# Load order of the last four summed weight tiles in a hybrid attention block

## The chip, the core and the metric

The kernel runs on one core of one Trainium2 chip. The metric is the time of one execution in microseconds (us) as the device reports it; the median of several executions stands for a kernel. A profile shows one execution on that core: PE is TensorE with its matmuls (PEld its weight loads), DVE is VectorE, ACT is ScalarE, POOL is GpSimd, and SP is the engine whose queue starts almost every DMA here.

## What is computed

The reference is one encoder layer: one input projection, two kinds of attention, gating, an output projection and a layer norm. Cut to what matters:

```python
h = x @ w_in                      # x (1024, 1024), w_in (1024, 3328)
q_a, k_a, v_a, z_a, q_b, k_b, v_b, z_b = split(h)
y_a = neighborhood_attention(q_a, k_a, v_a, rel_pos_bias)   # 8 heads of 64, 8 x 16 window on a 16 x 64 grid
y_b = windowed_gqa_with_sink(rotary(q_b), rotary(k_b), v_b, sink_logits)  # 8 query heads, 2 key heads, |i-j| <= 128
mixed = concat([y_a * silu(z_a), y_b * silu(z_b)])
x = layer_norm(2 ** 0.25 * x + mixed @ w_out, ln_gain, ln_bias)
```

## The kernel before

Accuracy comes from splitting float32 operands into a high and a low 16-bit part and adding three products. To split a weight tile the kernel must first know a power-of-two scale that keeps it in range, and that scale comes from sums of absolute values. This bookkeeping is what the change touches.

**Tiling.** The columns of `w_in` other than the values are cut into 21 column tiles of 128 columns, in the order of the list `ORDER`. Each tile is projected for two halves of the 1024 tokens, with 8 blocks of 128 rows and three products each: 48 matmuls of 128x512, line 401. The value columns are projected at the start in float32 (line 482).

**Two sorts of tiles.** The first six (`NPRO`, the names `zb0, z0, zb1, kb, qb0, z1`) are projected in the prologue, each with a scale of its own: as they are loaded (`wr`, line 192), ACT scans each half of a tile (`w_scan`, line 233), and `w_scale` turns the sums into the scale with a small matmul against a matrix of ones (lines 248 and 250) and five small DVE instructions (251 to 255). For the gate tiles among them (`ZPRO`, the tiles 0, 1, 2 and 5) sums by single column are needed too: `z_tree` adds up the scanned copies on DVE (lines 238 to 240) before the matmul of line 248.

The other 15 tiles (`NS`) are projected later, between the attention's own matmuls, and share one scale. So the prologue loads all of them as `ws0` to `ws14` (`sum_load`, line 641, 512 KB each), and sums their absolute values (`sum_w`): on ACT at line 670, on ACT at line 663 for the four gate tiles in `ZSUM` = 1, 5, 13 and 14, whose scanned copies go into the buffer `junk` that `w_scan` uses too, and on DVE at line 659 for tiles 4 and 7. The last eight tiles (`NR`) stay in their buffers and are split from there, much later (lines 203, 208 and 209); the others are loaded again when their turn comes.

**What sets the order.** In the prologue the program is written out by hand: `run_to` counts matmuls of line 401, and `at(c, fn)` puts a piece of work behind matmul number c. The sums stand at 14, 28, and so on up to 210, one for every 14 matmuls. Each sum, when it is placed, issues the load that stands four further on in the list of loads; the first four loads stand ahead of all sums. An engine executes its instructions in the order of the program, and so does the SP queue: a load behind a waiting one waits with it. The sum places run over the tiles 0 to 10 and then 13, 11, 14, 12, by a small table in the line that places them. The loads run over 0 to 14. The scale of the common group is computed behind matmul 219 from all 15 sums.

**Buffers.** The tiles `ws` rotate through eight buffers of the pool tag `big2`. Eight later tiles take the same buffers in the same rotation: four pairs of split output weights (`wo`, line 989) and the split gated results `m` of four head pairs (line 1015). A later tile waits until the last reader of the tile in its buffer is done.

Of the kernel before, what the change touches and what calls it, by code (L numbers as in the profile page):

```python
# [31 lines left out]
NS = 21 - NPRO  # L32
ZPRO = (0, 1, 2, 5)
ZSUM = (1, 5, 13, 14)
DSUM = (4, 7)
NR = 8
FILL = ORDER[NPRO:]
FILL_AT = [0, 8, 17, 25, 33, 41, 49, 57, 66, 74.5, 82.5, 91, 99, 107, 114, 121.5, 124, 126, 128, 131, 136]
# [27 lines left out]
def hybrid_block(ctx, tc, xT, x, wt, wv, wo, bias, sink, gain, lbias, cos, sin, bmask, out):  # L66
# [20 lines left out]
    def big_tile(name, shape=(128, 2, 512), dt=F32R):  # L87
        n = taken[0]
        taken[0] += 1
        tag = "big" if n < 8 or 16 <= n < 24 or n >= 32 + NS else "big2"  # L90
        return big.tile(list(shape), dt, tag=tag, name=name)
# [94 lines left out]
    NH = 2 * len(ORDER)  # L186
    NL = NH - 2 * NR

# [36 lines left out]
    def z_abs(n):  # L225
        return junk[:, S * (zabs[n] % 2):S * (zabs[n] % 2) + S]
# [206 lines left out]
    with ExitStack() as vctx:  # L433
# [201 lines left out]

        sums = {}

        def sum_load(i):
            if i < NS:
                sums[i] = big_tile(f"ws{i}", (128, 2, 4, 128), F32)  # L640
                nc.sync.dma_start(sums[i], wt[NPRO + i].rearrange("h p k c -> p h k c"))

# [7 lines left out]
            j = ZSUM.index(n - NPRO)  # L650
            nc.vector.tensor_reduce(zc[:, j:j + 1], zps.pop(n)[:, :128], axis=AXX, op=ALU.max)

        def sum_w(i):
            t, c = sums[i].rearrange("p h k c -> p (h k c)"), 2 * NPRO + i
            if i >= NS - NR:
                for h in range(2):
                    raws[2 * (NPRO + i) + h] = sums[i][:, h]
            if i in DSUM:
                nc.vector.tensor_reduce(wm[:, c:c + 1], t, axis=AXX, op=ALU.add, apply_absolute_value=True)
            elif i in ZSUM:  # L660
                n = NPRO + i
                zabs[n] = len(zabs)
                nc.scalar.activation(z_abs(n), t, AF.Abs, accum_out=wm[:, c:c + 1])
                if i == ZSUM[-1]:
                    at(ran[0] + 70, z_tree, n)
                else:
                    for d, fn in ((23, z_tree), (47, z_sum), (51, z_max)):
                        at(ran[0] + d, fn, n)
            else:
                nc.scalar.activation(scrap, t, AF.Abs, accum_out=wm[:, c:c + 1])  # L670
            sum_load(i + 4)

        def at(c, fn, *a):
            events.setdefault(c, []).append(lambda: fn(*a))
# [43 lines left out]
        for i in range(4):  # L718
            sum_load(i)
        for i in range(NS):  # L720
            at(14 + 14 * i, sum_w, {11: 13, 12: 11, 13: 14, 14: 12}.get(i, i))
        at(219, w_scale, NPRO)
        fill.extend(project(n) for n in ORDER[:NPRO])
        run_to(100)
# [139 lines left out]
    def quad(q):  # L864
        g, p, j, t, _ = units[4 * q]
        return g, p, j, t // 4 if g == "b" else t[0] // 2
# [315 lines left out]
    for i in range(-LD, NU + LO):  # L1182
# [61 lines left out]
        if 0 <= q < NU // 4:  # L1244
            g, p, j, h = quad(q)
# [90 lines left out]
```

## Time and profile before

| | |
|---|---|
| median of 3 runs | 449.64 us (449.15 to 450.77) |
| the profiled execution | 449.93 us, span from first to last instruction 448.1 us |
| PE busy | 439.5 us, 98% of the span |
| DVE, ACT, POOL busy | 344.6 us (77%), 304.1 us (68%), 229.3 us (51%) |
| HBM traffic over the span | 140 GB/s |
| granted TensorE clock, mean | 0.996 |

The profiled execution's own time is 1.8 us more than its span: that lies before the first and behind the last instruction. PE is nearly always busy, so where PE is kept waiting matters more than how busy the rest is. The ends of matmuls are modelled, 0.38 us for one of 128x512 where the next one starts 0.22 us after it, so a short stall of PE can hide in a busy row; starts are safer to read.

### The profile page before, as it was taken

To read this page: it belongs to the slowest core of one execution; us is meant where nothing else is said; L and a number is where in the kernel's file an instruction comes from. 1 tells how busy PE (TensorE), PEld (TensorE's weight loads), DVE (VectorE), ACT (ScalarE), POOL (GpSimd) and SP (SyncE) were. 2 spreads that over 40 slices of the span, in tenths; PEclk is the share of its full clock that TensorE was granted. 3 is DMA by queue.
4 is the path that set the end of the run, shared out by engine and by line. 5 is a ranking of instruction groups with operands and counts; after the bars stand their busy time and mean duration, and the time that the engine had idled before them with its cause. 6 is when DMAs were issued, how large, how long until landed. Compare 5 with 4: busy or idle time off the path is not lost.

```text
span 448.1 us, 9544 instructions
## 1 busy us (share of the span) xinstructions
PE 439.5 (98%) x3269; PEld 262.8 (59%) x3269; DVE 344.6 (77%) x857; ACT 304.1 (68%) x704; POOL 229.3 (51%) x244
## 2 busy tenths in 40 slices
PE   8999999998999999999999999999999999999994
PEld 8999974443445555565655565656555654444442
DVE  5787987927989787786898888897777746179954
ACT  5638749858578998888988978797886886002211
POOL 0003942563837838868516729667753555005840
PEclk9999999999999999999999999999999999999998
DMA  8897377985848888887888999999999878101721
GB/s 249 285 313 275 96 255 241 279 280 197 304 148 166 146 153 164 173 141 136 163 161 185 177 191 193 191 181 236 195 193 226 157 191 325 49 0 70 248 82 70
DMA packets 135136, 83.86 MB, mean 187 GB/s; under 512 B 101424, under 2 KB 113456, under 8 KB 134832
## 3 DMA queue, kind: packets, MB, share of 16 engines
q1 hardware_dynamic: 134656, 82.77, 75.8%
q8 instruction: 25, 0.41, 0.4%
q10 hardware_dynamic: 432, 0.49, 0.3%
q14 instruction: 23, 0.19, 0.1%
HBM read 52.83 MB, written 9.96 MB: 140 GB/s over the span
## 4 chain that ended last, share of the span: by engine, by line
PE 87%; POOL 4%; issue 4%; DMA 3%; DVE 1%; SPq 1%; ACT 1%; POOLq 0%; ACTq 0%; DVEq 0%
PE ps_pj L401 39%; PE ps_s L1033 9%; PE ps_t L886 7%; PE ps_s L482 6%; PE ps_pj L1033 5%; PE ps_t L1033 5%; PE ps_s L821 4%; PE ps_s L822 4%; PE ps_pj L482 3%; PE ps_t L482 3%; POOL wl L209 2%; PE ps_t L906 2%; DMA ws<-in_wt 1%; DMA wvraw<-in_wv 1%; POOL wr L208 1%
## 5 line engine op out<-in xcount | busy, mean ns | idle before, releaser
L401 PE MATMUL ps_pj<-xf,wh 128*128 128x512 f16 x672 | 202.6, 379 | 0.0
L401 PE MATMUL ps_pj<-xf,wl 128*128 128x512 f16 x336 | 127.3, 379 | 0.0
L401 PEld LDWEIGHTS <-wh 128*128 128x128 f16 x672 | 63.8, 98 | 61.7 <-issue 1.8
L847 ACT ACTIVATE ps_s<-sn,nm 128x385 f32<-128x385 f32 (+3 forms) x128 | 70.0, 547 | 29.6 <-DVE nm L831 28.6
L858 DVE SCALAR_TENSOR_TENSOR split<-ps_s,split 128x384 f16<-128x384 f32 (+2 forms) x128 | 65.6, 512 | 17.2 <-ACT split L857 16.3
L1033 PEld LDWEIGHTS <-m 128*128 128x128 f16 x408 | 38.8, 98 | 42.7 <-issue 0.2
L857 ACT ACTIVATE split<-ps_s 128x384 f16<-128x384 f32 (+2 forms) x128 | 57.6, 450 | 2.4
L401 PEld LDWEIGHTS <-wl 128*128 128x128 f16 x336 | 32.9, 98 | 36.7
L831 DVE CUSTOM_DVE_ANT_0 sn<-ps_s,bias,sg 128x264 f32<-128x264 f32 (+1 forms) x64 | 35.2, 550 | 16.0 <-PE ps_s L822 5.9
L208 POOL TENSOR_SCALAR wr<-wr,wsc 128x512 f32<-128x512 f32 x26 | 21.8, 840 | 42.4 <-ACT wh L203 36.8
L1033 PE MATMUL ps_s<-wo,m 128*128 128x512 f16 (+1 forms) x192 | 42.0, 372 | 0.0
L831 DVE CUSTOM_DVE_ANT_0 sn<-ps_s,bm,nsk 128x384 f32<-128x384 f32 (+1 forms) x64 | 40.7, 636 | 1.5 <-PE ps_s L822 1.3
L793 POOL TENSOR_SCALAR bias<-bias,rsg 128x552 f32<-128x552 f32 (+1 forms) x24 | 18.7, 779 | 40.2 <-DMA bias<-in_bias 35.4
L821 PE MATMUL ps_s<-ks,qs 128*128 128x384 f16 (+4 forms) x128 | 39.2, 306 | 0.0
L822 PE MATMUL ps_s<-ks,qs 128*128 128x384 f16 (+4 forms) x128 | 39.2, 306 | 0.0
L886 PEld LDWEIGHTS <-tr 128*128 128x128 f16 (+1 forms) x1104 | 36.6, 98 | 2.2
L209 POOL TENSOR_TENSOR wl<-wr,wh 128x512 f16<-128x512 f32 x26 | 32.2, 1240 | 2.2
L1090 ACT ACTIVATE sd<-mv,eps 128x1 f32<-128x1 f32 x8 | 2.4, 295 | 45.1 <-DVE mv L1088 42.8
L1132 POOL TENSOR_TENSOR xr<-xr,gb 128x512 f32<-128x512 f32 x7 | 11.2, 1607 | 41.1 <-ACT xr L1129 41.1
L482 PE MATMUL ps_s<-wvh,x 128*128 128x320 f32 x128 | 29.4, 310 | 0.0
L315 POOL COPY ks<-ks 64x512 f16<-64x512 f16 x40 | 26.0, 662 | 4.7 <-DVE ks L285 1.8
L1033 PE MATMUL ps_pj<-wo,m 128*128 128x512 f16 (+1 forms) x120 | 25.2, 347 | 0.0
(187 smaller groups left out, 827.8 us busy)
## 6 DMA issues: line engine op xcount, KB each, us to landing
xraw<-in_xT SPq DMA_DIRECT2D x31, 256.0 KB, 4.4
ws<-in_wt SPq DMA_DIRECT2D x15, 512.0 KB, 5.2
wr<-in_wt SPq DMA_DIRECT2D x26, 256.0 KB, 3.0
bias<-in_bias SPq DMA_DIRECT2D x16, 276.0 KB, 3.5
wor<-in_wo SPq DMA_DIRECT2D x16, 256.0 KB, 3.3
xr<-in_x SPq DMA_DIRECT2D x8, 512.0 KB, 9.0
out<-xr SPq DMA_DIRECT2D x14, 256.0 KB, 2.1
bias<-in_bias SPq DMA_DIRECT2D x8, 368.0 KB, 3.8
```

The lines of the kernel that those rows point to most:

```text
L208: nc.gpsimd.tensor_scalar(raw, raw, scale, 1.0, op0=ALU.mult, op1=ALU.mult)
L209: nc.gpsimd.tensor_sub(l, raw, h)
L401: nc.tensor.matmul(ps, a[:, k % 4, :], mv, start=(k == 0 and i == 0), stop=(k == KT - 1 and i == 2))
L482: nc.tensor.matmul(ps[:, :320], lh[t // 4, k][:, ts], rh[k][:, cs], start=(k == 0 and i == 0), stop=(k == KT - 1 and i == 2))
L821: nc.tensor.matmul(ps[:, :m], q, sl[0], start=True, stop=False)
L822: nc.tensor.matmul(ps[:, :m], q, sl[1], start=False, stop=True)
L831: nc.vector.tensor_tensor_reduce(sn[:, :m], ps[:, :m], bias_t, sg[:, c:c + 1], init, op0=ALU.add, op1=ALU.min, accum_out=nm)
L847: nc.scalar.activation(pt[:, :m], sn[:, :m], AF.Exp, bias=nm, scale=-1.0, accum_out=sm[:, k:k + 1])
L857: nc.scalar.activation(hl[:, :m, 0, :c], src, AF.Copy, scale=PSCALE)
L858: nc.vector.scalar_tensor_tensor(hl[:, :m, 1, :c], src, PSCALE, hl[:, :m, 0, :c], op0=ALU.mult, op1=ALU.subtract)
L886: nc.tensor.matmul(ps[:, HD * m:HD * m + HD], a, b_, start=(i == 0), stop=(i == len(mms) - 1))
L1033: nc.tensor.matmul(ps, lh[:, ts], rh[:, cs], start=(e == EO[0] and i == 0), stop=(e == EO[-1] and i == 2))
```

## The change

The order of the sums becomes a list, `SUMS`, and both the loads and the sums go through it. Before, the places of the sums were permuted and the loads were not.

```diff
+SUMS = list(range(11)) + [13, 11, 14, 12]
...
-        def sum_load(i):
-            if i < NS:
+        def sum_load(j):
+            if j < NS:
+                i = SUMS[j]
                 sums[i] = big_tile(f"ws{i}", (128, 2, 4, 128), F32)
                 nc.sync.dma_start(sums[i], wt[NPRO + i].rearrange("h p k c -> p h k c"))
...
-        def sum_w(i):
+        def sum_w(j):
+            i = SUMS[j]
             t, c = sums[i].rearrange("p h k c -> p (h k c)"), 2 * NPRO + i
...
-            sum_load(i + 4)
+            sum_load(j + 4)
...
         for i in range(NS):
-            at(14 + 14 * i, sum_w, {11: 13, 12: 11, 13: 14, 14: 12}.get(i, i))
+            at(14 + 14 * i, sum_w, i)
```

A second effect lies in the old `sum_load(i + 4)`: its argument was the tile's number, not the place of the sum. For the sums of tiles 0 to 10 the two are the same, and these issue all remaining loads, so no load is added or lost.

On SP, at the place where the last of these loads are issued, the kernel before has these rows (`ws` are the summed tiles with their numbers, `wr` halves of the prologue's tiles, `vwin` a copy of the values in device memory; a number behind the underscore is that of the buffer object, in the order of allocation):

```order
L641 DMA ws10_1125<-in_wt 128x2x512
L192 DMA wr12_1171<-in_wt 128x512
L641 DMA ws11_1178<-in_wt 128x2x512
L641 DMA ws12_1199<-in_wt 128x2x512
L641 DMA ws13_1219<-in_wt 128x2x512
L192 DMA wr13_1238<-in_wt 128x512
L641 DMA ws14_1252<-in_wt 128x2x512
L192 DMA wr14_1262<-in_wt 128x512
L738 DMA vwin0_76<-vd_75 64x6144
```

And this is the same place with the change (its line numbers are up to three higher):

```order
L643 DMA ws10_1125<-in_wt 128x2x512
L193 DMA wr12_1171<-in_wt 128x512
L643 DMA ws13_1178<-in_wt 128x2x512
L643 DMA ws11_1199<-in_wt 128x2x512
L643 DMA ws14_1219<-in_wt 128x2x512
L193 DMA wr13_1238<-in_wt 128x512
L643 DMA ws12_1252<-in_wt 128x2x512
L193 DMA wr14_1262<-in_wt 128x512
L741 DMA vwin0_76<-vd_75 64x6144
```

The queue has the same rows at the same places; four of them carry another tile. Tile 13 goes from the third of the four places to the first, tile 11 from the first to the second, tile 14 from the fourth to the third and tile 12 from the second to the fourth. The buffer objects 1178, 1199, 1219 and 1252, and so the places in the rotation, go with the place in the queue.

On ACT, where these tiles are summed, the kernel before has these rows (`rp_raw` is a projected half tile read out of PSUM for the rotary step, `wh` a high part):

```order
L331 ACTIVATE rp_raw_1276<-ps_pj_1240 128x512
L663 ACTIVATE junk_123,wm_108<-ws13_1219 128x1024
L233 ACTIVATE junk_123,wm_108<-wr11_1119 128x512
L670 ACTIVATE scrap_128,wm_108<-ws11_1178 128x1024
L331 ACTIVATE rp_raw_1327<-ps_pj_1280 128x512
L203 ACTIVATE wh10_1330<-wr10_1032,wsc_110 128x512
```

And with the change:

```order
L332 ACTIVATE rp_raw_1276<-ps_pj_1240 128x512
L666 ACTIVATE junk_123,wm_108<-ws13_1178 128x1024
L234 ACTIVATE junk_123,wm_108<-wr11_1119 128x512
L673 ACTIVATE scrap_128,wm_108<-ws11_1199 128x1024
L332 ACTIVATE rp_raw_1327<-ps_pj_1280 128x512
L204 ACTIVATE wh10_1330<-wr10_1032,wsc_110 128x512
```

The order of the sums stands as it was: tile 13, then the scan of the second half of prologue tile 5 (`wr11`), then tile 11. Only the buffers that they read have changed. PE and DVE have the same rows in both kernels.

## The prediction

> **What bounds the kernel now.** I read the page first, then the list of waits of PE and ACT, then the chain of waits around the one wait that mattered, and last the timeline there.
>
> ```profile
> span 448.1 us, 9544 instructions
> PE 439.5 (98%) x3269; PEld 262.8 (59%) x3269; DVE 344.6 (77%) x857; ACT 304.1 (68%) x704; POOL 229.3 (51%) x244
> ...
> PE ps_t L248 <- DVE cs L240: 1.6, 1, 1.6
> PE ps_t L1115 <- ACT dg L1114: 1.5, 1, 1.5
> PE ps_t L441 <- DVE warm L438: 1.0, 1, 1.0
> PE ps_pj L482 <- DVE x L453: 0.3, 1, 0.3
> ...
> ACT junk L663 <- DMA ws<-in_wt: 2.6, 1, 2.6
> ```
>
> PE is the bound: it is busy for 439.5 of 448.1 us. The four PE rows are all its waits on other engines, each with the total, the number of times and the longest. Three belong to the warm-up, the first tiles and the last normalisation, which this change does not touch. The remaining one, 1.6 us at line 248, is a wait in the middle. The ACT row is the only wait of any engine for a `ws` load, 2.6 us, once. The chain of waits ties the two together (start, duration, what):
>
> ```profile
> 94.17 0.43 SPq L641
> ...
> 94.65 0.46 SPq L641
> ...
> 95.15 6.71 DMA ws<-in_wt
> ...
> 103.03 0.62 ACT junk L233 x2
> ...
> 103.67 0.44 DVE junk L238
> ...
> 104.46 0.24 DVE cs L240
> ...
> ```
>
> Three `ws` loads are issued in a row, at 94.17, 94.65 and 95.15. The third is tile 13 and lands at 95.15 + 6.71 = 101.86. ACT then sums it (line 663), scans the last half of prologue tile 5 behind it (line 233), and only then can DVE add up the columns (lines 238 to 240) and PE run the matmul of line 248, with which the chain goes on. So PE's wait is not for the tile that came late: it is for the scan that is queued behind the late tile's sum on ACT.
>
> **What the change moves.** Tile 13's load goes from the third of these places in the SP queue to the first. Tile 11 goes to the second, tile 14 to the third, tile 12 to the fourth, behind a 256 KB load. Nothing is added or removed, all four loads are 512 KB, and SP passes the same number of rows, so the queue itself costs the same. What changes is when each tile lands. The landing of the other places comes from the issues in short stretches of the trace (the last number is us to landing; the stretches hold the first, the second and the fourth place):
>
> ```profile
> ws<-in_wt SPq DMA_DIRECT2D x1, 512.0 KB, 4.5
> ws<-in_wt SPq DMA_DIRECT2D x1, 512.0 KB, 5.9
> 97.26 0.43 SPq L641 DMA_DIRECT2D ws<-in_wt  x1
> ws<-in_wt SPq DMA_DIRECT2D x1, 512.0 KB, 6.7
> ```
>
> First place 94.17 + 4.5 = 98.7, second 94.65 + 5.9 = 100.5, third 101.9, fourth 97.26 + 6.7 = 104.0. In these rows the loads land in the order of issue. I take it that the places keep their landing times, since size and queue are the same: tile 13 then lands at 98.7, 3.2 us earlier.
>
> Now what ends last in its place. The timeline (in brackets the idle time before, and its cause):
>
> ```profile
> 98.69 0.60 ACT L331 ACTIVATE rp_raw<-ps_pj 128x512 f32<-128x512 f32 x1 [1.62 <-PE ps_pj L401]
> 101.88 1.06 ACT L663 ACTIVATE junk<-ws 128x1024 bf16<-128x1024 f32 x1 [2.59 <-DMA ws<-in_wt]
> 101.42 0.69 DVE L335 TENSOR_TENSOR rp_raw<-rp_raw,rp_sw 128x512 f32<-128x512 f32 x1
> 103.67 0.43 DVE L238 TENSOR_TENSOR junk<-junk 128x512 bf16<-128x512 bf16 x1 [1.56 <-ACT junk L233]
> 102.38 0.59 PE L401 MATMUL ps_pj<-xf,wh 128*128 128x512 f16 x2
> 102.81 0.38 PE L401 MATMUL ps_pj<-xf,wl 128*128 128x512 f16 x1
> 104.74 0.22 PE L248 MATMUL ps_t<-cs,ones 128*128 128x128 bf16 x1 [1.55 <-DVE cs L240]
> ```
>
> ACT is free at 98.69 + 0.60 = 99.29, after tile 13 has landed, so the sum starts at 99.29 and the 2.59 us vanish on ACT. From the start of the sum to the start of line 238 it was 103.67 - 101.88 = 1.79 us; the scan would thus let DVE start at 101.08. But DVE is in the rotary step of line 335 until 101.42 + 0.69 = 102.11. **DVE becomes the limit**: it gains 103.67 - 102.11 = 1.56 us, its whole idle time there. From line 238 to the matmul it is 104.74 - 103.67 = 1.07 us, so PE starts line 248 at 102.11 + 1.07 = 103.18. Without any wait it could start 0.22 us after the matmul of 102.81 (the pair at 102.38 takes 0.43 for two starts), at 103.03. PE's true stall of 1.71 us shrinks to 0.15, and the gain is **1.56 us**, bounded above by 1.71.
>
> The other three tiles. The sum of tile 11 followed that of tile 13 by 103.55 - 101.88 = 1.67 us; it would start at 100.96, and its data lands at 100.5, 0.4 us before. If it lands later, ACT waits, at a place where it has time: it next waits for PE. The last two sums, and what uses them:
>
> ```profile
> 103.55 1.04 ACT L670 ACTIVATE scrap<-ws 128x1024 bf16<-128x1024 f32 x1
> ...
> 105.64 0.60 ACT L331 ACTIVATE rp_raw<-ps_pj 128x512 f32<-128x512 f32 x1 [0.96 <-PE ps_pj L401]
> ...
> 108.02 1.06 ACT L663 ACTIVATE junk<-ws 128x1024 bf16<-128x1024 f32 x1
> 109.69 1.04 ACT L670 ACTIVATE scrap<-ws 128x1024 bf16<-128x1024 f32 x1
> 110.63 0.19 ACT L670 ACTIVATION_READ_ACCUMULATOR scrap<-ws 128x1 f32 x1
> ...
> 111.32 0.17 PE L250 MATMUL ps_t<-wm,ones 128*128 128x15 bf16 x1
> ```
>
> All of these follow PE (the row at 105.64 waits for a matmul group), so they move 1.56 us ahead: tile 14 is needed at 106.5 and lands at 101.9, tile 12 at 108.1 and lands at 104.0. Both are covered, by 4 us. The matmul of line 250 keeps its 0.5 us behind the last sum.
>
> **Does the gain reach the end?** No later row of PE's list waits on anything between here and the last normalisation, and there PE is waited for. What could hold it is work that does not move with PE. DMA traffic from before the stall stays where it is, but it has run out before the next loads, as two stretches of 1 us show (the last two columns are DMA share and GB/s):
>
> ```profile
> 106.00:107.00 1.00, 1.00 (x7) 0.44 (x5) 0.93 (x5) 1.00 (x3) 0.06 (x1) 1.00 0.00 0
> 108.00:109.00 1.00, 1.00 (x6) 0.49 (x5) 0.97 (x2) 0.98 (x2) 0.94 (x2) 1.00 0.00 0
> ...
> 123.48 0.63 ACT L430 ACTIVATE scrap<-wos 128x512 bf16<-128x512 f32 x1 [2.82 <-DMA wos<-in_wo]
> 125.74 0.69 DVE L362 SCALAR_TENSOR_TENSOR z<-z,ps_pj 128x512 f32<-128x512 f32 x1
> 126.48 0.59 PE L401 MATMUL ps_pj<-xf,wh 128*128 128x512 f16 x2
> ```
>
> No transfer runs there, so later loads can start 1.56 us earlier. The tight place is 126.48: PE's next group takes the PSUM bank that DVE's line 362 releases at 126.43, 0.05 us before. ACT's wait at 123.48 for a `wos` load stands ahead of it. Since that load is issued behind POOL work that follows ACT and DVE, I take it to move along.
>
> The buffers' later users change too. The third `m` tile now waits for the split of tile 13 instead of tile 11, and the third `wo` pair for tile 14 instead of tile 13:
>
> ```profile
> 317.77 1.16 POOL L209 TENSOR_TENSOR wl<-ws,wh 128x512 f16<-128x512 f32 x1
> 330.90 1.16 POOL L209 TENSOR_TENSOR wl<-ws,wh 128x512 f16<-128x512 f32 x1
> 346.10 0.60 ACT L1015 CAST m<-z 128x512 f16<-128x512 f32 x1
> 361.66 2.55 ACT L989 ACTIVATE wo<-wor,wos 128x512 f16<-128x512 f32 x4
> ```
>
> Tile 13's last split ends at 318.9 and the third `m` is written at 346.1, with 27 us between; tile 14's ends at 332.1 and the `wo` pair is written from 361.7. I cost this at nothing.
>
> **Sum.** The profiled execution took 449.93 us: 449.93 - 1.56 = 448.37. It stands 0.29 above the median of 449.64, so for a median I take 449.64 - 1.56 = **448.1 us**.
>
> [...]
>
> **The rivals.** (1) *The load lands late in its new place.* For: over all 15 loads the time to land goes up to 6.9 us.
>
> ```profile
> DMA to landing us min/median/max: 4.0/5.2/6.9
> ```
>
> With 6.9 us tile 13 lands at 101.07, and the gain is 101.86 - 101.07 = 0.8 us: 448.8 us; as late as now, 449.6. Against: the long landings quoted above are those of the third and fourth place, behind other loads, and the first place has 4.5. (2) *The gain is given back at 126.48.* If the `wos` load ahead of ACT's line 430 keeps its absolute landing, the gate's evacuation and DVE's line 362 stay, and PE waits for its bank what it gained: 449.6 us, no change. Against: the empty DMA queue. (3) *The change does not do what it says to PE*: another wait stands right behind, for example the load of the scan behind the sum; again about 449.6. Against: that load stands ahead of all these in the SP queue, and in the chain the scan's rows come with no wait of their own. (4) *Slower: tile 12 pays.* It now goes last. If it lands after 108.1, ACT's last sum is late, and 0.5 us further on PE's line 250 stalls one for one, and with it all of PE's queue. It decides from a landing at 108.6; the gain is used up at 110.2, and 0.5% of loss needs 112.4, which is 15 us after the issue, against 6.7 in the trace: 452 us or more.
>
> **How the numbers follow.** The forecast gets 0.73, rival (1) 0.10, (2) and (3) together 0.11, (4) 0.06. About 0.5%, or 2.2 us, is what a measurement of this kernel can tell from no change: the three runs before span 1.6 us. The mechanism cannot give 2.2 us, since PE's stall is 1.71; a measured time under 447.4 would take 0.7 us of scatter on top of the forecast, to which I give 0.14. Over 451.9 I give 0.06, from (4). The rest, 0.80, is within 0.5%. The forecast alone would span 447.2 to 448.9; with rivals (1) to (3) the range is 447.2 to 449.8.
>
> **What would show it.** Right: no wait of ACT line 666 (the old 663) for a `ws` load; ACT's sum of tile 13 at about 99.3; DVE's line 238 directly behind its line 336, without idle time; PE's line 249 (the old 248) at about 103.2 and hardly a wait; all of PE 1.5 us earlier from there, and a span near 446.5. Wrong: a wait on ACT for the first of the sums (rival 1), PE's start at 126.48 unmoved (2), a wait of ACT's last sum or PE's line 251 for tile 12 (4), or a gain at 105 us that is gone by 360 us.

## The result, and the profile after

The changed kernel took 448.06 us as a median of 10 runs (447.59 to 450.27), the kernel before 450.24 us in the 10 runs beside it. The ratio is 0.9954, with a 95% interval of 0.9932 to 0.9977: 0.5% faster, where the prediction had 1.56 us or 0.35%. A second set of 12 runs, at a later time, gave 0.9968 (0.9950 to 0.9985).

The waits of PE in the changed kernel (engine and what it waited for; us in total, times, longest):

```profile
PE ps_t L1118 <- ACT dg L1117: 1.5, 1, 1.5
PE ps_t L442 <- DVE warm L439: 1.0, 1, 1.0
```

The wait at line 248 (now 249) is gone. The one ACT wait for a `ws` load has moved to the tile that is summed second, as the view of that tile shows:

```profile
its engine sat idle before it (us, times) until:
  DMA ws<-in_wt: 0.6, 1
who waited for it (us, times):
  ACT scrap L673: 0.6, 1
```

The timeline of the changed kernel at the place that the prediction worked out:

```profile
93.67 1.45 SPq L643 DMA_DIRECT2D ws<-in_wt  x3
...
98.21 0.60 ACT L332 ACTIVATE rp_raw<-ps_pj 128x512 f32<-128x512 f32 x1 [1.62 <-PE ps_pj L402]
98.70 1.05 ACT L666 ACTIVATE junk<-ws 128x1024 bf16<-128x1024 f32 x1
...
99.75 0.61 ACT L234 ACTIVATE junk<-wr 128x512 bf16<-128x512 f32 x1
...
100.93 0.69 DVE L336 TENSOR_TENSOR rp_raw<-rp_raw,rp_sw 128x512 f32<-128x512 f32 x1
...
101.10 1.06 ACT L673 ACTIVATE scrap<-ws 128x1024 bf16<-128x1024 f32 x1 [0.65 <-DMA ws<-in_wt]
...
101.54 0.42 DVE L239 TENSOR_TENSOR junk<-junk 128x512 bf16<-128x512 bf16 x1
...
102.33 0.38 PE L402 MATMUL ps_pj<-xf,wl 128*128 128x512 f16 x1
102.60 0.22 PE L249 MATMUL ps_t<-cs,ones 128*128 128x128 bf16 x1
...
122.15 0.63 ACT L431 ACTIVATE scrap<-wos 128x512 bf16<-128x512 f32 x1 [3.64 <-DMA wos<-in_wo]
```

Tile 13's sum starts right behind the read-out of line 332, without a wait. DVE's line 239 follows line 336 without idle time. PE starts line 249 0.27 us after the matmul ahead of it, 0.05 us more than the usual 0.22.

The whole execution is 2.1 us shorter (spans of 446.0 and 448.1 us), but not all of it is the wait. The row of line 332 is a mark of the same work ahead of the wait: it started at 98.69 before and 98.21 now, so 0.48 us of the difference was there already, from the start of the kernel, where the change does nothing. From this mark to the matmul it was 104.74 - 98.69 = 6.05 us and is 102.60 - 98.21 = 4.39: the wait gave **1.66 us**. Nothing took it back later: from line 248 (now 249) to the end of the span it is 448.1 - 104.74 = 343.4 us before and 446.0 - 102.60 = 343.4 with the change.

### The profile page after: what moved, and what is told of

Read it like the earlier page. It is cut to its first block, busy times and chain, and to the rows that moved or that the text cites. A ratio compares the mean times of both kernels' runs of the same rounds, so it can differ in the third digit from the quotient of the medians.

```text
span 446.0 us, 9544 instructions
## 1 busy us (share of the span) xinstructions
PE 439.2 (98%) x3269; PEld 262.9 (59%) x3269; DVE 344.3 (77%) x857; ACT 303.9 (68%) x704; POOL 229.2 (51%) x244
## 4 chain that ended last, share of the span: by engine, by line
PE 98%; DVE 0%; ACT 0%; issue 0%; ACTq 0%
PE ps_pj L402 49%; PE ps_s L1036 9%; PE ps_t L889 7%; PE ps_s L483 6%; PE ps_pj L1036 5%; PE ps_t L1036 5%; PE ps_s L824 4%; PE ps_s L825 4%; PE ps_pj L483 3%; PE ps_t L483 3%; PE ps_t L909 2%; PE ps_t L442 1%; PE ps_t L1118 0%; DVE xr L1113 0%; ACT xr L1122 0%
```

## The experiments

Each kernel ran beside the kernel before on the same chip; ratios are to that.

**Is it the order of the loads, or the scan behind the sum?** The loads keep their old order, and tile 13's sum is placed one matmul later, behind the scan:

```diff
-            at(14 + 14 * i, sum_w, {11: 13, 12: 11, 13: 14, 14: 12}.get(i, i))
+            at(14 + 14 * i + (i == 11), sum_w, {11: 13, 12: 11, 13: 14, 14: 12}.get(i, i))
```

> The loads keep the old order; only ACT's order changes: the scan of prologue tile 5's last half stands ahead of tile 13's sum. Theory (PE waited for the scan that was queued behind the late sum): ACT still waits about 2 us for tile 13's load, now behind the scan, but PE's wait at line 248 falls from 1.55 us to under 0.3, and the time falls by 1.5 to 2.1 us, ratio to before near 0.996, as with the change. Rival (the order of the loads itself helps, by DMA traffic or otherwise): no gain, ratio 1.000.

Ratio 0.9957 (0.9937 to 0.9977). The timeline of ACT and PE:

```profile
98.80 0.62 ACT L233 ACTIVATE junk<-wr 128x512 bf16<-128x512 f32 x1
...
101.11 1.06 ACT L663 ACTIVATE junk<-ws 128x1024 bf16<-128x1024 f32 x1 [1.60 <-DMA ws<-in_wt]
...
102.70 0.22 PE L248 MATMUL ps_t<-cs,ones 128*128 128x128 bf16 x1
```

ACT still waits for tile 13, 1.6 us, and PE does not wait at line 248 at all. The gain needs no new load order; it needs the scan not to stand behind a late load. The same run shows a wait of PE that the profile of before does not have:

```profile
123.41 0.63 ACT L430 ACTIVATE scrap<-wos 128x512 bf16<-128x512 f32 x1 [5.05 <-DMA wos<-in_wo]
...
124.04 0.67 ACT L361 ACTIVATE z<-ps_pj,invt 128x512 f32<-128x512 f32 x1
...
124.74 0.69 DVE L362 SCALAR_TENSOR_TENSOR z<-z,ps_pj 128x512 f32<-128x512 f32 x1 [1.38 <-ACT z L361]
...
125.48 0.59 PE L401 MATMUL ps_pj<-xf,wh 128*128 128x512 f16 x2 [0.90 <-DVE z L362]
```

It is the same pattern: ACT waits 5.05 us for an output-weight tile, the evacuation of a gate tile stands behind it, DVE's line 362 behind that, and PE waits 0.9 us for the PSUM bank. From line 248 to the end of the span this execution takes 447.1 - 102.70 = 344.4 us, 1.0 more than the 343.4 of the others.

**How early must the tile be?** The loads run through a list of their own, `LOADS`, and the sums as before:

```diff
+LOADS = list(range(11)) + [11, 13, 12, 14]
...
-        def sum_load(i):
-            if i < NS:
+        def sum_load(j):
+            if j < NS:
+                i = LOADS[j]
```

> Tile 13 is loaded in the second of the four places (11, 13, 12, 14). Theory: it lands between the first and the third place, 100.5 by the profile of before and about 1 us later by that of the change, so ACT still waits 1.2 to 2.3 us, PE's wait is 0.1 to 1.3 us, and the gain is a part of the whole, 0.3 to 1.4 us, ratio 0.997 to 0.999. Rival (any landing ahead of the third place gives the whole gain, since DVE is busy until 102.1): ratio 0.9955 and no wait of PE. Rival (the order of the loads does not matter): ratio 1.000 with a wait of 1.5 us.

Ratio 0.9967 (0.9946 to 0.9989). In the profile ACT waits 0.88 us, and PE's line 249 starts at 102.67 without idle time, as with the change:

```profile
99.77 1.06 ACT L665 ACTIVATE junk<-ws 128x1024 bf16<-128x1024 f32 x1 [0.88 <-DMA ws<-in_wt]
...
101.62 0.42 DVE L239 TENSOR_TENSOR junk<-junk 128x512 bf16<-128x512 bf16 x1
...
102.67 0.22 PE L249 MATMUL ps_t<-cs,ones 128*128 128x128 bf16 x1
```

The theory missed: it had 1.2 to 2.3 us of wait for ACT and 0.1 to 1.3 for PE. In this execution the first rival holds: DVE is busy until then, so 0.9 us of lateness is free. The load of the second place landed at 99.75 here and at 101.08 in the profile of the changed kernel, where tile 11 had that place; so late, the scan would have let DVE start at 101.10 + 1.79 = 102.89 there instead of 101.54, and PE would have lost 1.3 us. The intervals do not tell second and first place apart.

**The other way.** The same edit with `[11, 12, 14, 13]`:

> Tile 13 is loaded in the last of the four places (11, 12, 14, 13), the other way from the change. Theory: it lands about 2 us after the third place (104.0 against 101.9), and ACT's scan, DVE and PE move one for one: PE's wait at line 248 is 3.2 to 4.2 us and the time rises by 1.6 to 2.6 us over before, ratio 1.0035 to 1.006. Rival (the gain of the change is not this wait, or PE catches up later): ratio 1.000, or a longer wait without a longer span.

Ratio 1.0092 (1.0064 to 1.0121), 455.11 us: about twice the loss that the theory had. The wait was 4.27 us, just over the range; what was not expected stands in the stretches of 2 us behind it (busy time and instructions of PE, PEld, DVE, ACT and POOL; then the granted clock, DMA share and GB/s):

```profile
104.99 1.06 ACT L665 ACTIVATE junk<-ws 128x1024 bf16<-128x1024 f32 x1 [5.32 <-DMA ws<-in_wt]
107.85 0.27 PE L249 MATMUL ps_t<-cs,ones 128*128 128x128 bf16 x1 [4.27 <-DVE cs L241]
...
104.00:106.00 2.00, 0.00 (x0) 0.00 (x0) 0.00 (x0) 1.01 (x2) 0.00 (x0) 0.99 0.56 236
106.00:108.00 2.00, 0.15 (x2) 0.15 (x2) 0.94 (x3) 1.79 (x6) 0.00 (x0) 0.50 0.03 12
108.00:110.00 2.00, 2.00 (x6) 0.67 (x5) 1.64 (x9) 0.57 (x2) 0.00 (x0) 0.50 0.00 0
110.00:112.00 2.00, 2.00 (x6) 0.76 (x5) 1.93 (x6) 1.95 (x5) 1.19 (x2) 0.50 0.00 0
112.00:114.00 2.00, 2.00 (x9) 0.79 (x8) 1.97 (x2) 2.00 (x4) 1.93 (x2) 0.80 0.03 3
...
116.86 0.17 PE L251 MATMUL ps_t<-wm,ones 128*128 128x15 bf16 x1
```

The granted clock falls to one half and stays there until almost 113. From line 249 to line 251 it is 116.86 - 107.85 = 9.01 us; in the kernel before, the same work from line 248 to line 250 took 111.32 - 104.74 = 6.58. So the stall cost 2.4 us more than its length: PE worked at half the clock from 107.85 to about 112.8, and half of these 4.95 us is 2.5.

**The scatter of the kernel before.**

> The kernel before, unchanged, for a second profile and the scatter. Theory: PE waits at line 248 again, for as long as tile 13 lands late, and that landing differs between executions by about 1 us, so the wait is 1.0 to 3.0 us; ratio 1.000 within 0.25%. If the wait is 1.55 us again to within 0.1, the landing does not scatter, and the 0.5 us by which PE was ahead in the changed kernel before the wait is scatter of the start. If the wait were absent here, the first profile would have been an accident, and the change could not owe its gain to it.

Ratio 0.9979 (0.9958 to 1.0001) between two sets of the same kernel, and a wait of only 0.93 us: under the range expected. In the kernel before's 29 runs beside these, nine had a granted clock of 0.993 or less and took 451.9 to 453.1 us. That raised the question whether these executions, too, had a long wait at line 248.

**Again, with more kernels side by side.**

> The changed kernel, unchanged, beside the other kernels of this job. Theory: no wait of PE at line 249 (old 248) or under 0.3 us, no execution with a granted clock under 0.996, median 447.8 to 448.6 us, ratio to before 0.994 to 0.9975. Rival (the 0.46% of the first comparison was mostly scatter between sets of executions, as the 0.2% between two sets of the kernel before suggests): ratio above 0.9975.

> The kernel before once more, to see its scatter. In the last job 9 of 29 executions of it had a granted clock of 0.992 to 0.993 and took 451.9 to 453.1 us, and none of 12 of the second set. Theory (PE's wait at line 248 is longer in these and halves the clock for some us, as the fourth-place run showed for a wait of 4.3 us): the executions fall into two groups again, those with a clock of 0.996 and more under 451.5 us, those with less above it; a profile of the second group would show a wait over 2.5 us. Rival (the slow group has nothing to do with this wait): such executions occur for the changed kernels in this job as well.

Ratios 0.9968 (0.9950 to 0.9985) and 1.0001 (0.9979 to 1.0022). The changed kernel had no wait of PE at line 249 and no clock under 0.996, a median of 448.29 us. The kernel before had one execution in 12 with a clock of 0.992, at 452.75 us, and in the 34 runs beside it four with 0.993 or less; two more, of 452.4 and 452.6 us in the 29 and the 34 runs, had 0.996, which the split by clock does not explain. The profiled one had a wait of 1.16 us and a mean clock of 0.998.

**Can either late load be kept from PE for good?** First the scan of the output-weight tile alone, moved behind the evacuation, in the changed kernel; then, in a second kernel, also the tile scan ahead of tile 13's sum, as in the first experiment:

```diff
-            at(231 + 10 * i, wo_pre, i)
+            at(276 if i == 3 else 231 + 10 * i, wo_pre, i)
```

> The changed kernel with ACT's scan of the fourth output-weight tile moved from matmul 261 to 276, behind the evacuation of gate tile 5's first half. Theory (the PE wait of 0.9 us seen in the scan-first run, at the PSUM bank behind DVE's line 362, comes from that scan waiting for a late load ahead of the evacuation): ACT still waits for the load, 1 to 4 us, but PE never waits for the bank. In an execution where the load is not late this brings nothing; so the median is 0 to 0.5 us under that of the changed kernel in this job, and the upper end of its times comes down. Rival (the executions of the changed kernel above 449.5 us come from the start of the kernel, where PE waits 0 to 0.6 us for its first tiles): the same median and the same upper end.

> The changed kernel with both scans moved: the scan of prologue tile 5 ahead of tile 13's sum, and the output-weight scan behind the evacuation. Theory: neither late load can reach PE; no PE wait between the first tiles and the last normalisation, the time is that of the changed kernel's good executions, 447.6 to 448.3 us as a median, ratio 0.994 to 0.997. Rival (moving tile 13's sum one place back delays something else, such as the sum of tile 11 and the common scale): a PE wait at line 251 (old 250) or a median above the changed kernel's.

Medians of 448.21 and 448.26 us against 448.29 of the changed kernel beside them; both ratios 0.9960 (0.9944 to 0.9976 and 0.9945 to 0.9976). The upper end of the times stayed near 450 (450.0 and 449.9 against 450.25). Neither is measurably better than the change. In the profile of the first, the gate's evacuation runs 3 us ahead of the scan, and PE has no wait for the bank:

```profile
119.41 0.69 ACT L362 ACTIVATE z<-ps_pj,invt 128x512 f32<-128x512 f32 x1 [0.60 <-PE ps_pj L402]
122.53 0.63 ACT L431 ACTIVATE scrap<-wos 128x512 bf16<-128x512 f32 x1
```

But ACT did not wait for the output-weight load either, in this profile or in the second kernel's, where the theory had 1 to 4 us: at its later place the scan came behind the landing. So these profiles do not show a late load being kept from PE, and the profiles of the changed kernel itself have no wait for the bank. The executions near 450 us must come from elsewhere. The start of the kernel, as the rival has it, was not changed in any run; the table further down shows how far it scatters.

**Does a longer wait bring the low clock?** The kernel before with one or two more ACT passes over tile 13 behind its sum, whose results nobody uses (`range(2 ...)` in the second):

```diff
                 nc.scalar.activation(z_abs(n), t, AF.Abs, accum_out=wm[:, c:c + 1])
+                for _ in range(1 if i == 13 else 0):
+                    nc.scalar.activation(scrap, t, AF.Abs)
```

> The kernel before with one more ACT pass over tile 13 (1.0 us, its result unused) between tile 13's sum and the scan that PE waits for. Theory (what stands on ACT between the late load and the scan reaches PE one for one, and a stall of about 2.5 us is near the point where the granted clock halves): PE's wait at line 248 is 1.0 us longer than in the kernel before, 1.9 to 2.7 us. Executions whose clock stays at 0.996 and more take 1.0 us more, 450.3 to 451.5 us; the others have 0.993 or less and take 452.5 to 454 us, and they are more frequent than in the kernel before (14 of 87 so far). Rival (the clock has nothing to do with this wait): as many low clocks as before, and all times 1.0 us up.

> The same with two more passes, 2.0 us. Theory: PE's wait is 2.9 to 3.7 us, the granted clock halves behind it in most executions, as in the fourth-place run, and the time is 453 to 455 us, that is 2.0 us for the wait and about 2 us for the clock. Rival (no link to the clock): 2.0 us over the kernel before, 451.5 to 452.5 us, and a clock of 0.996 and more.

The 2.5 us at which the first expects the clock to halve is the author's estimate; in the fourth-place run it halved 2.4 us after PE's last matmul. Ratios 1.0027 (1.0004 to 1.0050) and 1.0070 (1.0046 to 1.0094). The profiles show waits of 2.5 and 2.8 us. In both the matmuls of line 401 start 0.22 us apart behind the wait, as ahead of it, and the mean clock is 0.997 and 0.999, so it did not halve there:

```profile
105.82 0.22 PE L248 MATMUL ps_t<-cs,ones 128*128 128x128 bf16 x1 [2.48 <-DVE cs L240]
```

```profile
106.11 0.22 PE L248 MATMUL ps_t<-cs,ones 128*128 128x128 bf16 x1 [2.81 <-DVE cs L240]
```

The first wait is in the range expected, the second just under it, since ACT's own wait for tile 13 was only 1.8 us there. With one pass two of 10 executions had a clock of 0.993 or less, no clear rise over the kernel before, and with two passes six of 10, as the theory had it. Their medians were 452.5 and 453.4 us, against 450.7 and 451.3 for the others of the same kernel. One of the others, with 0.996, took 453.9 us, outside both groups of the theory.

> One look at the kernel before. Theory: if the execution took over 451.8 us, the profile shows a wait over 2 us at line 248 and a granted clock of about one half for some us behind it; if under, a wait of 0.9 to 1.6 us and a full clock. Rival: a slow execution with a wait of 1.6 us or less.

> A second look, with the same expectation: over 451.8 us goes with a wait over 2 us and a halved clock behind line 248, under it with 0.9 to 1.6 us and a full clock. Rival: a slow execution with a wait of 1.6 us or less.

They took 449.45 and 449.82 us, with waits of 1.01 and 1.17 us and a mean clock of 0.999 in both: as expected for that side, and no execution of the other side was caught.

All counts of executions with a granted clock of 0.993 or less, by how late the scan could run (the kernel before's 10 runs of the first comparison have no clock listed and are left out):

| kernels | profiled waits of PE at line 248 | low clock |
|---|---|---|
| changed (two sets), scan first, second place, both with the moved output-weight scan | none in their profiles | 0 of 69 |
| before (three sets beside others, two of its own) | 0.9 to 1.6 us | 15 of 106 |
| one more pass | 2.5 us | 2 of 10 |
| two more passes | 2.8 us | 6 of 10 |
| fourth place | 4.3 us | 4 of 6 |

The share rises with the wait and is zero where PE does not wait. That a low-clock execution of the kernel before has a longer wait than the profiled ones is what this fits, but none was profiled, so it is not shown. The mean clock is also a blunt sign. In the first profile of the kernel before it is 0.996 only because of the last 3.56 us, at half the clock with PE done (columns as in the stretches above):

```profile
444.58:448.14 3.56, 0.00 (x0) 0.00 (x0) 0.00 (x0) 0.00 (x0) 0.00 (x0) 0.50 0.39 147
```

An execution that spent as long at half the clock in the middle, and was at full clock to its end, would have the same mean, 1 - 0.5 x 3.56 / 448.1 = 0.996. So the three long executions with 0.996 may belong to the others; that is not shown either.

**Where the profiles differ.** The 14 profiles can be cut at two marks, the row of line 331 (now 332) ahead of the wait and the matmul of line 248 (now 249) behind it:

| profiles | line 331 at, us | from there to line 248 | from there to the end |
|---|---|---|---|
| before (five) | 98.65 to 100.02 | 5.43 to 6.05 | 343.4 |
| changed (two), second place, both with the moved output-weight scan | 98.21 to 98.76 | 4.38 to 4.39 | 343.4 |
| scan first | 98.31 | 4.39 | 344.4 |
| one more pass, two more passes | 98.84, 98.81 | 6.98, 7.30 | 343.4 |
| fourth place | 99.08 | 8.77 | 345.8 |

The first column is set in the first 11 us, where all these kernels are alike: from the 61st matmul, which starts between 9.57 and 11.37 us, to the mark it is 88.64 to 88.66 us in all 14. The latest start, that of the second profile of the kernel before, goes with matmuls of line 482 that start 0.27 us apart until 8.3 us and 0.15 from 8.7 us on; in the first they start 0.15 us apart from 5.4 us on. So the start alone moves the time by up to 1.8 us. All else that differs lies in the wait, in the bank in the scan-first run and in the clock in the fourth-place run.

## Why the prediction was right

- **What bounds.** Right: the wait at line 248 was for the scan queued behind tile 13's sum on ACT. The scan-first kernel shows it, with the loads in the old order.
- **Where tile 13 lands.** Right in what matters: it lands before ACT is free. That the places keep their landing times was too simple. The second place's load took 5.9 us in the profile of before; in that of the change it was issued 0.48 us into the row at 93.67 and landed at 101.08, 6.9 us later. So tile 11, forecast to land 0.4 us early, came 0.65 us late. As the prediction had it, ACT has time there, and nothing followed from it.
- **DVE as the new limit.** Right: line 239 follows line 336 at once. It starts 0.61 us after the start of line 336, not the 0.69 of its duration: the rows of DVE overlap a little, and so do those of ACT, where tile 13's sum starts 0.49 us after a row of 0.60. So the stall's rest is 0.05 us instead of 0.15, and the gain 1.66 instead of 1.56.
- **Tiles 14 and 12, the buffers.** Right: ACT's last sums and PE's line 251 do not wait, and neither does the third `m` tile.
- **Whether the gain reaches the end.** Right in the profile: PE has no wait between line 249 and the last normalisation, and both kernels take 343.4 us from there to the end. But the reason given, that the output-weight load moves along, held only in part. ACT's wait for it grew from 2.82 to 3.64 us, and in the scan-first run the second rival took 0.9 us. That rival deserved its place.
- **The size.** Right for the profile on which it rests, 1.66 us against 1.56. That the measured 448.06 us meets the forecast of 448.1 so closely is luck. The forecast started from 449.64, but beside the changed kernel the kernel before took 450.24, so the median fell by 2.2 us, 0.6 more than forecast. The forecast also treated one profiled wait as the wait of every execution, and that profile had the longest of five: by the table the wait's part is 1.0 to 1.7 us. Two other parts lie in the difference of the medians. One is the start: the two profiles of the changed kernel reach the mark 0.27 us or more ahead of all five of the kernel before. No work differs there, and with the moved scans the mark came at 98.50 and 98.76, so this is chance as far as is known. The other is the 15 executions of the kernel before with a low clock, of a median of 452.4 us; the 91 with 0.994 or more have 449.75, 1.56 us above the 448.19 of the changed kernel's 22. What the sum left out is the clock: in the fourth-place run a PE wait of 4.27 us cost 2.4 us more than its length. The prediction's statement that the mechanism cannot give 2.2 us, since PE's stall is 1.71, holds for an execution with that stall and a full clock. Whether a longer wait stands behind the 15 others was not caught in a profile.

## What to carry to other kernels

Follow a wait of the bound engine back through the queue of the engine that it waits for: the instruction that comes late may be ready itself and only stand behind another one's late load. It can be freed from either side, by an earlier load or by putting the urgent instruction first; an earlier load needs to be no earlier than the next limit, here DVE. Take the landing of a queued load from several profiles, and reckon that a stall of TensorE can cost more than its length: here one of 4.3 us cost 2.4 us on top, while the profiled ones of 2.5 and 2.8 us cost no more than they lasted.

## What the runs showed of the hardware

**The granted clock halved in a stall of 4.27 us.** In the fourth-place run PE's last matmul ended at 107.85 - 4.27 = 103.58, and the granted clock fell near 106, after 2.4 us without a matmul:

```profile
105.50:106.00 0.50, 0.00 (x0) 0.00 (x0) 0.00 (x0) 0.50 (x2) 0.00 (x0) 0.97 0.12 49
106.00:106.50 0.50, 0.00 (x0) 0.00 (x0) 0.00 (x0) 0.50 (x3) 0.00 (x0) 0.50 0.06 25
...
112.50:113.00 0.50, 0.50 (x3) 0.23 (x2) 0.50 (x1) 0.50 (x3) 0.47 (x1) 0.70 0.00 0
113.00:113.50 0.50, 0.50 (x4) 0.21 (x3) 0.50 (x1) 0.50 (x2) 0.46 (x1) 1.00 0.00 0
```

It came back near 112.8, about 5 us after PE had resumed. Until then the matmuls of line 402 start 0.43 us apart, and 0.22 us apart from 112.9 on. The profiled stalls of 2.48 and 2.81 us, with one and two more passes, are longer than the 2.4 us after which the clock fell here, but the matmuls of line 401 behind them start 0.22 us apart. So in these three profiles the length of the stall alone does not decide. What else does was not shown: this is the one fall of the clock that a profile has ahead of PE's last matmul.

**Landings scatter.** Over five profiles of the kernel before, tile 13's load took 6.1 to 6.7 us to land from the same place in the queue, ACT's wait for it was 2.0 to 2.6 us and PE's 0.9 to 1.6. The profile on which the prediction rests had the longest of all three.
